# Key and query stores moved to GpSimd's queue, and three loads that are asked for at other places, in a one-core hybrid decoder layer

## The chip, the cores and the metric

One NeuronCore of a Trainium2 chip runs the whole program. The metric is device microseconds of one execution; the kernel was timed in three runs. Five engines work side by side, each through its own list of instructions in order: TensorE (PE; its weight loads are PEld), VectorE (DVE), ScalarE (ACT), GpSimd (POOL) and SyncE (SP), which here only issues transfers. Transfers issued by SP appear in the profile as queue q1 (hardware_dynamic), those issued by GpSimd as queue q0 (software_dynamic).

## The reference

One layer of a decoder with two groups of heads, 1024 tokens behind 16 meta tokens, D_MODEL 1024:

```python
u = rmsnorm(h, attn_norm_w[l])
proj = u @ w_in[l]
gq, gk, gv, gz, gb, ga, fq, fk, fv, ff = jnp.split(proj, IN_SPLITS, axis=-1)
o_gdn = gated_deltanet_group(jnp.concatenate([gq, gk, gv], axis=-1), gz, gb, ga, ...)  # 4 heads, chunked delta rule
o_fox = forgetting_attention_group(fq, fk, fv, ff, fgate_b[l])                         # 8 heads, softmax with forget bias
h = h + jnp.concatenate([o_gdn, o_fox], axis=-1) @ w_out[l]
h = h + swiglu(rmsnorm(h, ffn_norm_w[l]), w_gate[l], w_up[l], w_down[l])
```

and a last rmsnorm. "gdn" below is the delta-rule group, "fox" the attention group.

## The kernel before

Everything is float32 and every matrix product is made of three: each operand is split into a high part (a CAST on ACT, `whi_`, `uh`) and the rest (a subtraction on DVE, `wlo_`, `ul`), by the helper `split`. The stages follow one another on PE; the ones that matter here, with their place in the profiled execution:

- **Value projection** (about 232 to 287 us, tiles `fv`). `fox` goes over two blocks of weights, b = 1 and then 0, and in each over nine token tiles, t = -1 to 7. A tile is 24 matmuls into one of three PSUM banks; ACT and DVE split it into `fvt` (three buffers) and SP stores it to `v_d`. Inside the loop `fox_load` asks for the weights of the next block: it loads two halves (`raw_fv`, then `raw_fk`), and ACT and DVE split them. At the same time DVE inverts 32-row blocks for the delta rule (`invert`, L533 and L535, tile `up`), a long row of small instructions.
- **Key and query projection** (287 to 436 us, tiles `pj_fk` and `pj_fq`). `fox_proj` makes four row blocks m of three pieces each, for keys and then for queries: 24 matmuls, then ACT (L777) and DVE (L778) split the piece into `fhl`, which has two buffers, and L780 stores it to DRAM (`k_d`, `q_d`), whence the attention loads it later. The query pieces are named by their first column, 16, 358 and 700. A piece's ACT instruction waits until the store of the piece two before it has landed, since it writes the same buffer. PE writes the pieces, and after them the `wog` tiles, into three PSUM banks in turn, so that a group of matmuls needs the piece three before it to be split.
- **Delta rule.** In between, `levels` builds the inverses (its loads `ubk` and `na` come from DRAM), and from 349 us on `scan` runs eight chunks: four loads each (`ra`, `rb`, `rc`, `zt`), on PE `p`, `pvn`, `pd`, `po` and `ot`, on DVE `r` (L836) and `s` (L853), on POOL `sg` (L848) and a power for the norm (`os`, L220).
- **Attention** (from 439 us). `att_head` loads a head (`ka`, `qa`, `kk`, `sa`, `avt`, `vm`), PE makes scores (`sc`) in two PSUM banks, DVE (L1030) adds the mask and takes the minimum, ACT exponentiates into `pr` and copies the columns of the meta tokens into `pm` (L1040). As filler between them runs `wout_gdn`: the gdn half of the output projection in tiles `wog`, each with a residual tile `ht` that is loaded from x, added on DVE (L1190) and stored to `h_d`.
- After 666 us come the FFN products, in which PE has no gaps.

PE's order is written by hand through a planner (`PeOrder`, with chains, due times and a filler); the order on the other engines and queues is set when the program is built, by a scheduler that simulates the program and takes `tc.issue_after(x)` as a request that an instruction be placed behind x. A wait at run time comes only from data and from buffers. Each transfer that POOL issues carries one of eight semaphores in turn.

Of the kernel before, what the change touches and what calls it, by code (L numbers as in the profile page):

```python
# [9 lines left out]
F32 = mybir.dt.float32  # L10
# [11 lines left out]
NT = S // P  # L22
# [75 lines left out]
def tile_hymba_layer(ctx, tc, x, meta, attn_norm_w, w_in, conv_w, a_log, dt_bias, gdn_norm_w,  # L98
                     fgate_b, w_out, ffn_norm_w, w_gate, w_up, w_down, final_norm_w, out):
    nc = tc.nc  # L100
    x, out, w_in, conv_w = x[0], out[0], w_in[0], conv_w[0]
# [12 lines left out]
    def ps_mm(name):  # L114
        rot[0] = rot[0] % 3 + 1 if rot[0] else 0
        return ps_v(name) if rot[0] > 1 else bank("mm", 1, name)
# [46 lines left out]
    def split(dst_hi, dst_lo, src, col=None):  # L163
        if col is None:
            cast = nc.scalar.copy(dst_hi, src)  # L165
            low = nc.vector.tensor_sub(dst_lo, src, dst_hi.bitcast(F32))  # L166
        else:
            cast = nc.scalar.activation(dst_hi, src, AF.Copy, scale=col)
            low = nc.vector.scalar_tensor_tensor(dst_lo, src, col, dst_hi.bitcast(F32),
                                                 op0=ALU.mult, op1=ALU.subtract)  # L170
        tail[0] = (cast, low)
        return cast
# [37 lines left out]
    def mm3g(dst, pairs, us):  # L210
        n = len(pairs)
        for i, (lh, ll, rh, rl) in enumerate(pairs):
            for a, b, first, last in ((lh, rh, i == 0, False), (lh, rl, False, False), (ll, rh, False, i == n - 1)):
                nc.tensor.matmul(dst, a, b, start=first, stop=last)  # L214
                od.pe(us)
                yield
# [56 lines left out]
    def tok_cols(t):  # L273
        return (0, NM) if t < 0 else (NM + P * t, P)
# [30 lines left out]
    def gate_out(t, acc, pool, tag, h0):  # L305
        zt = pool.tile([P, 4, 2, DH], F32, tag=tag, name=f"zt{h0}_{t}")
        zt = zt.rearrange("p a b c -> p (a b c)")[:, :256].rearrange("p (h c) -> p h c", h=2)
        nc.scalar.activation(zt, acc[:, :256].rearrange("p (h c) -> p h c", h=2), AF.Silu)
        return nc.sync.dma_start(rec_d[t, :, 7, h0:h0 + 2], zt)
# [291 lines left out]
    def levels(hp):  # L601
        na = lp.tile([P, 2, NT, P], F32, tag="na", bufs=2, name=f"na_{hp}")
        tb = lp.tile([P, 2, NT, 32], F32, tag="tb", bufs=2, name=f"tb_{hp}")
        ubk = lp.tile([P, 2, NT, 32], F32, tag="ubk", bufs=2, name=f"ubk_{hp}")
        with tc.issue_after((last[0] or vst[0]).ins):
            nc.sync.dma_start(ubk, ud_d[hp].rearrange("b j h t k -> (b j) h t k"))
            for i in range(2):
                nc.sync.dma_start(na[:, i], rec_d[:, :, 0, 2 * hp + i].rearrange("t p c -> p t c"))
# [97 lines left out]
    def proj_tmg(acc, t, w, n):  # L706
        col, rows = tok_cols(t)
        yield from mm3g(acc[:rows, :n], [(uh[:, k, col:col + rows], ul[:, k, col:col + rows], w[0][k][:, :n],
                                          w[1][k][:, :n]) for k in range(KT)], n / 2400)

    last, vst = [None], [None]
# [5 lines left out]
    def fox_load():  # L717
        if fox_ws:
            with tc.issue_after(vst[0].ins) if vst[0] and not last[0] else nullcontext():
                fox_w.append(win_block(*fox_ws.pop(0)))  # L720

    t_ld, hds, fixed, fq_m, h_ld = [], {}, [], [0], {}
# [39 lines left out]
    def fox_proj(dst, chunks, off, scale, nm):  # L762
        for b in range(2):
            w = fox_w.pop(0)
            for i in range(2):
                m = 2 * b + i
                for ci, (c0, n) in enumerate(chunks):
                    if (i, ci) == (0, 1):
                        fox_load()
                    acc = ps_mm(f"pj_{nm}{m}_{c0}")  # L770
                    yield from mm3g(acc[:, :n], [(w[0][k][:, P * i:P * i + P], w[1][k][:, P * i:P * i + P],
                                                  uh[:, k, c0:c0 + n], ul[:, k, c0:c0 + n])
                                                 for k in range(KT)], n / 2400)
                    od.on("act", n / 1200)
                    od.on("dve", n / 900)
                    hl = fp.tile([P, 2, 348], F32R, tag="fhl", name=f"fhl_{nm}{m}_{c0}")
                    nc.scalar.activation(hl[:, 0, :n], acc[:, :n], AF.Copy, scale=scale)  # L777
                    nc.vector.scalar_tensor_tensor(hl[:, 1, :n], acc[:, :n], scale, hl[:, 0, :n].bitcast(F32),  # L778
                                                   op0=ALU.mult, op1=ALU.subtract)
                    last[0] = nc.sync.dma_start(dst(m)[:, :, c0 - off:c0 - off + n], hl[:, :, :n].bitcast(F32))  # L780
                    if off:
                        fq_m[0] = m

# [28 lines left out]
    ra_ld = {}  # L812
# [116 lines left out]
    def fox():  # L929
        fox_load()  # L930
        w = fox_w.pop(0)
        for t in range(NT):
            if t == 1:
                fox_load()
            acc = ps_mm(f"z0_{t}")
            yield from proj_tmg(acc, t, w, 256)
            gate_out(t, acc, *((fvp, "fvt") if t < NT - 2 else (fp, "fhl")), 0)
        for b in (1, 0):
            n = 256 + 8 * b
            w = fox_w.pop(0)  # L940
            for t in range(-1, NT):
                if t == 1:
                    fox_load()
                col, rows = tok_cols(t)
                acc = (ps_mm if b or t % 2 else ps_t)(f"fv{b}_{t}")
                yield from proj_tmg(acc, t, w, n)
                vt = fvp.tile([P, 4, 2, DH], F32R, tag="fvt", name=f"fvt{b}_{t}")
                av = acc[:rows, :256].rearrange("p (h d) -> p h d", d=DH)
                split(vt[:rows, :, 0], vt[:rows, :, 1], av)
                src = vt[:rows].rearrange("p h a d -> p h (a d)").bitcast(F32)  # L950
                if t < 0:
                    for j in range(GRP):
                        vst[0] = nc.sync.dma_start(
                            vz_d[4 * b:4 * b + 4, VZ * j:VZ * j + NM * 512].rearrange(
                                "h (r f) -> r h f", f=512)[:, :, 0:P], src)
                else:
                    vst[0] = nc.sync.dma_start(v_d[4 * b:4 * b + 4, col:col + rows].rearrange("h t d -> t h d"), src)
                if b:
                    nc.vector.tensor_copy(fr[:rows, NT if t < 0 else t], acc[:rows, 256:264])
        fvc.close()  # L960
        yield from fox_proj(lambda m: k_d[m], TCH, 0, 1.0, "fk")
        od.add(csum(), od.t + 8.0)
        yield from fox_proj(lambda m: q_d[m].rearrange("a p c -> p a c"), ((NM, 342), (NM + 342, 342), (NM + 684, 340)), NM, -DH ** -0.5, "fq")

    lv_left, outs_left = {0, 1}, set(range(NT))
    for hp in range(2):
        od.add(levels(hp), LV0[hp] - 20.0)
# [179 lines left out]
    h_d = dram.tile([NT, P, D], F32, name="h_d")  # L1147
# [17 lines left out]
    def wout_block(k0, nb, tiles=None, col=None):  # L1165
        ws = ([], [])
        for i in range(2):
            hl = load_w([(wout_w(k0 + 2 * i, nb), 1024)], f"wo{k0}_{nb}{i}", tiles and tiles(i), col)
            for o, t in zip(ws, hl):
                o.extend(t[:, 512 * k:512 * k + 512] for k in range(2))  # L1170
        return ws

    def gdn_pairs(tt, nb):
        a, b, (wh, wl) = og_of("h", tt), og_of("l", tt), wvs[nb]
        return [(a[:, k], b[:, k], wh[k], wl[k]) for k in range(4)]

    def wout_gdn(nb, tt):
        if nb not in wvs:
            parts_n[0] = 2 if nb else 1
            wvs[nb] = wout_block(0, nb, col=gnw)  # L1180
            parts_n[0] = 1
            od.on("act", 2.2)
            od.on("dve", 3.2)
        cols, nbc = slice(P * tt, P * tt + P), slice(512 * nb, 512 * nb + 512)
        ht = wo.tile([P, 512], F32, tag="ht", bufs=5, name=f"ht_{tt}_{nb}")
        with tc.issue_after(ra_ld[NT - 2].ins):
            (nc.gpsimd if len(t_ld) > 1 else nc.sync).dma_start(ht, x[cols, nbc])
        acc = ps_mm(f"wog_{tt}_{nb}")
        yield from mm3g(acc, gdn_pairs(tt, nb), 0.2135)
        V.tensor_add(ht, acc, ht)  # L1190
        nc.gpsimd.dma_start(h_d[tt, :, nbc], ht)
        yield od.on("dve", 0.6)

    tiles = [(nb, tt) for nb in range(2) for tt in range(NT)]
# [96 lines left out]
    with tc.issue_after(ofl[ORDER[1]].ins):  # L1291
        nc.sync.dma_start(nwb2, ffn_norm_w[0].partition_broadcast(P))
    pfp = woc.enter_context(tc.tile_pool(name="pf", bufs=1, side="right", reuse_waits="tile"))
    with tc.issue_after(h_ld[1].ins):
        wfs = [wout_block(4, 0)]
    rot[0] = 1
    for _ in wout_gdn(1, 1):
        pass
# [445 lines left out]
```

## Time and profile before

| | us |
|---|---|
| median of three runs (1304.51 to 1305.75) | 1305.42 |
| the profiled execution | 1304.52 |
| its span | 1302.8 |
| PE busy in the span | 1278.7 |
| DVE / ACT / POOL busy | 837.9 / 547.2 / 352.2 |

Between the span and the time of the profiled execution lie 1.7 us. In a row of the timeline the first number is the start in us, the second the duration, and the bracket at the end tells how long the engine sat idle before the instruction and whose end released it. In a row of the critical chain there is only start, duration and what. "SPq" rows are SP's issues; a row with x4 merges four. The granted clock of PE stands as a share of full speed (PEclk), the DMA share as the mean busy share of the 16 DMA engines.

### The profile page before, as it was taken

To read this page: it belongs to the slowest core of one execution; us is meant where nothing else is said; L and a number is where in the kernel's file an instruction comes from. 1 tells how busy PE (TensorE), PEld (TensorE's weight loads), DVE (VectorE), ACT (ScalarE), POOL (GpSimd) and SP (SyncE) were. 2 spreads that over 40 slices of the span, in tenths; PEclk is the share of its full clock that TensorE was granted. 3 is DMA by queue.
4 is the path that set the end of the run, shared out by engine and by line. 5 is a ranking of instruction groups with operands and counts; after the bars stand their busy time and mean duration, and the time that the engine had idled before them with its cause. 6 is when DMAs were issued, how large, how long until landed. Compare 5 with 4: busy or idle time off the path is not lost.

```text
span 1302.8 us, 19946 instructions
## 1 busy us (share of the span) xinstructions
PE 1278.7 (98%) x7434; PEld 1127.8 (87%) x7434; DVE 837.9 (64%) x1508; ACT 547.2 (42%) x940; POOL 352.2 (27%) x318
## 2 busy tenths in 40 slices
PE   9999999999999799999999999999999999999998
PEld 8999999999999788887778888888888888888887
DVE  6667898573257388886887666556666664365645
ACT  6455444142234377784553333233333343433332
POOL 2012213101222212112504534455334453020401
PEclk9999999999999899999999999999999999999999
DMA  6443624667499867748435644543444467945513
GB/s 230 132 118 110 186 83 106 175 193 221 148 331 258 243 185 190 212 101 258 166 114 161 196 166 157 185 158 134 157 157 162 162 218 264 397 179 193 208 67 129
DMA packets 185808, 234.90 MB, mean 180 GB/s; under 512 B 19160, under 2 KB 137904, under 8 KB 182896
## 3 DMA queue, kind: packets, MB, share of 16 engines
q1 hardware_dynamic: 182576, 224.20, 53.6%
q0 software_dynamic: 3136, 9.44, 2.5%
q8 instruction: 58, 0.95, 0.3%
q14 instruction: 38, 0.31, 0.1%
HBM read 154.68 MB, written 78.92 MB: 179 GB/s over the span
## 4 chain that ended last, share of the span: by engine, by line
PE 89%; DMA 5%; DVE 3%; issue 2%; ACT 1%; SPq 1%; POOL 0%; POOLq 0%; DVEq 0%; ACTq 0%
PE xp L1625 9%; PE yp L1625 7%; PE ua L1450 5%; PE ga L1450 5%; PE gb L1450 5%; PE ud L1450 5%; PE gd L1450 5%; PE ub L1450 5%; PE pj_fk L214 3%; PE pj_fq L214 3%; PE fv L214 2%; PE pt L1071 2%; PE ge L1450 2%; PE ue L1450 2%; PE z L214 2%; PE wog L214 2%
## 5 line engine op out<-in xcount | busy, mean ns | idle before, releaser
L166 DVE TENSOR_TENSOR al_p<-ra_p,ah_p 128x2048 fp32r<-128x2048 f32 (+1 forms) x21 | 46.6, 2221 | 93.8 <-ACT ah_p L165 93.8
L165 ACT CAST ah_p<-ra_p 128x2048 fp32r<-128x2048 f32 (+1 forms) x21 | 37.1, 1766 | 105.9 <-PE xp L1625 48.5
L1625 PE MATMUL xp<-wl_p,ah_p 128*128 128x512 f32 (+1 forms) x176 | 67.3, 382 | 0.0
L1625 PE MATMUL xp<-wh_p,al_p 128*128 128x512 f32 (+1 forms) x176 | 67.3, 382 | 0.0
L1625 PE MATMUL xp<-wh_p,ah_p 128*128 128x512 f32 (+1 forms) x176 | 67.3, 382 | 0.0
L1506 POOL TENSOR_TENSOR gzw<-gzw,uzt 128x512 f32<-128x512 f32 x11 | 18.1, 1650 | 165.2 <-DVE uzt L1495 139.4
L1450 PE MATMUL gb<-uh_p,w_g_p 128*128 128x512 f32 x176 | 57.8, 389 | 0.0
L1450 PE MATMUL gd<-uh_p,w_g_p 128*128 128x512 f32 x176 | 57.8, 389 | 0.0
L1450 PE MATMUL ud<-uh_p,w_u_p 128*128 128x512 f32 x176 | 57.8, 389 | 0.0
L1450 PE MATMUL ub<-uh_p,w_u_p 128*128 128x512 f32 x176 | 57.8, 389 | 0.0
L166 DVE TENSOR_TENSOR w_u_p<-raw_u,w_u_p 128x512 fp32r<-128x512 f32 x42 | 42.9, 1022 | 21.6 <-ACT w_u_p L165 21.5
L1506 POOL TENSOR_TENSOR gxy<-gxy,uxy 128x512 f32<-128x512 f32 x22 | 38.9, 1769 | 65.3 <-DVE uxy L1495 57.5
L165 ACT CAST ph<-pt 128x512 fp32r<-128x512 f32 (+1 forms) x96 | 45.4, 478 | 23.3 <-PE pt L1071 20.7
L166 DVE TENSOR_TENSOR pl<-pt,ph 128x512 fp32r<-128x512 f32 (+1 forms) x96 | 51.9, 552 | 4.5 <-ACT ph L165 4.0
L1035 ACT ACTIVATE pr<-pr,sm 128x144 f32<-128x144 f32 (+3 forms) x64 | 50.7, 793 | 8.1 <-DVE sm L1030 7.7
L1450 PE MATMUL ga<-uh_p,w_g_p 128*128 128x512 f32 x160 | 52.5, 389 | 0.0
L1450 PE MATMUL ua<-uh_p,w_u_p 128*128 128x512 f32 x160 | 52.5, 389 | 0.0
L1625 PE MATMUL yp<-wh_p,ah_p 128*128 128x512 f32 x132 | 51.3, 389 | 0.0
L1625 PE MATMUL yp<-wl_p,ah_p 128*128 128x512 f32 x132 | 51.3, 389 | 0.0
L1625 PE MATMUL yp<-wh_p,al_p 128*128 128x512 f32 x132 | 51.3, 389 | 0.0
L165 ACT CAST w_u_p<-raw_u 128x512 fp32r<-128x512 f32 x42 | 26.1, 620 | 55.4 <-PE gd L1450 33.6
L166 DVE TENSOR_TENSOR wl_p<-rw_p,wh_p 128x2048 fp32r<-128x2048 f32 (+1 forms) x21 | 46.9, 2234 | 3.4 <-ACT wh_p L165 3.4
(649 smaller groups left out, 4235.2 us busy)
## 6 DMA issues: line engine op xcount, KB each, us to landing
ra_p<-ao_p SPq DMA_DIRECT2D x14, 1024.0 KB
raw_g<-in_w_gate_dram SPq DMA_DIRECT2D x22, 512.0 KB
raw_u<-in_w_up_dram SPq DMA_DIRECT2D x22, 512.0 KB
raw_d<-in_w_down_dram SPq DMA_DIRECT2D x22, 512.0 KB
wt_p<-raw_d SPq DMA_DIRECT2D x33, 256.0 KB
rw_p<-wt_p SPq DMA_DIRECT2D x8, 1024.0 KB
rw_p<-in_w_down_dram SPq DMA_DIRECT2D x6, 1024.0 KB
ao_p<-gzw SPq DMA_DIRECT2D x22, 256.0 KB
```

The source lines that it names most:

```text
L165: cast = nc.scalar.copy(dst_hi, src)
L166: low = nc.vector.tensor_sub(dst_lo, src, dst_hi.bitcast(F32))
L214: nc.tensor.matmul(dst, a, b, start=first, stop=last)
L1035: nc.scalar.activation(pr[:, :n], pr[:, :n], AF.Exp, bias=sm[:, np_ - 1:np_], scale=-1.0, accum_out=rsum[:, h, j:j + 1])
L1071: nc.tensor.transpose(pt[:, P * j:P * j + P], pts[j][0][:, j, c0:c0 + P], ident)
L1450: nc.tensor.matmul(dst, a[:, c], b[:, k], start=(first and k == 0 and i == 0), stop=(k == 3 and i == 2), skip_group_check=not first)
L1506: last_mul[0] = G.tensor_tensor(gs[d], gs[d], us[d], op=ALU.mult)
L1625: nc.tensor.matmul(dst[:, n_], a[:, f, c], b[:, f, n_], start=(first and i == 0 and n == 0), stop=(i == NF - 1 and n == 2), skip_group_che ...
```

## The change

- In `fox_proj` the 24 stores of key and query pieces (L780) are issued by GpSimd and no longer by SP.
- In `fox`, in the first value block, the weights of the second are asked for at t = 3 (the fifth tile) and no longer at t = 1.
- In `levels` the three loads are placed behind the last value store that has been written down, no longer behind the last key store.
- In `wout_gdn` the load of a residual tile is placed behind the `h_d` store of the tile two before it. Before, all were placed behind a load of the scan, so that the first five stood together at the start and the others followed as their buffers came free.
- The fox half of the output weights (`wfs`, two loads `raw_wo` of 512 KB) is placed behind the loads of head 2, no longer of head 1.

```diff
--- before.py
+++ after.py
@@ -602,7 +602,7 @@
         na = lp.tile([P, 2, NT, P], F32, tag="na", bufs=2, name=f"na_{hp}")
         tb = lp.tile([P, 2, NT, 32], F32, tag="tb", bufs=2, name=f"tb_{hp}")
         ubk = lp.tile([P, 2, NT, 32], F32, tag="ubk", bufs=2, name=f"ubk_{hp}")
-        with tc.issue_after((last[0] or vst[0]).ins):
+        with tc.issue_after(vst[0].ins):
             nc.sync.dma_start(ubk, ud_d[hp].rearrange("b j h t k -> (b j) h t k"))
             for i in range(2):
                 nc.sync.dma_start(na[:, i], rec_d[:, :, 0, 2 * hp + i].rearrange("t p c -> p t c"))
@@ -777,7 +777,7 @@
                     nc.scalar.activation(hl[:, 0, :n], acc[:, :n], AF.Copy, scale=scale)
                     nc.vector.scalar_tensor_tensor(hl[:, 1, :n], acc[:, :n], scale, hl[:, 0, :n].bitcast(F32),
                                                    op0=ALU.mult, op1=ALU.subtract)
-                    last[0] = nc.sync.dma_start(dst(m)[:, :, c0 - off:c0 - off + n], hl[:, :, :n].bitcast(F32))
+                    last[0] = nc.gpsimd.dma_start(dst(m)[:, :, c0 - off:c0 - off + n], hl[:, :, :n].bitcast(F32))
                     if off:
                         fq_m[0] = m
 
@@ -939,7 +939,7 @@
             n = 256 + 8 * b
             w = fox_w.pop(0)
             for t in range(-1, NT):
-                if t == 1:
+                if t == (3 if b else 1):
                     fox_load()
                 col, rows = tok_cols(t)
                 acc = (ps_mm if b or t % 2 else ps_t)(f"fv{b}_{t}")
@@ -1174,6 +1174,8 @@
         a, b, (wh, wl) = og_of("h", tt), og_of("l", tt), wvs[nb]
         return [(a[:, k], b[:, k], wh[k], wl[k]) for k in range(4)]
 
+    h_st = []
+
     def wout_gdn(nb, tt):
         if nb not in wvs:
             parts_n[0] = 2 if nb else 1
@@ -1183,12 +1185,12 @@
             od.on("dve", 3.2)
         cols, nbc = slice(P * tt, P * tt + P), slice(512 * nb, 512 * nb + 512)
         ht = wo.tile([P, 512], F32, tag="ht", bufs=5, name=f"ht_{tt}_{nb}")
-        with tc.issue_after(ra_ld[NT - 2].ins):
-            (nc.gpsimd if len(t_ld) > 1 else nc.sync).dma_start(ht, x[cols, nbc])
+        with tc.issue_after(h_st[-2].ins) if len(h_st) >= 2 else nullcontext():
+            nc.gpsimd.dma_start(ht, x[cols, nbc])
         acc = ps_mm(f"wog_{tt}_{nb}")
         yield from mm3g(acc, gdn_pairs(tt, nb), 0.2135)
         V.tensor_add(ht, acc, ht)
-        nc.gpsimd.dma_start(h_d[tt, :, nbc], ht)
+        h_st.append(nc.gpsimd.dma_start(h_d[tt, :, nbc], ht))
         yield od.on("dve", 0.6)
 
     tiles = [(nb, tt) for nb in range(2) for tt in range(NT)]
@@ -1291,7 +1293,7 @@
     with tc.issue_after(ofl[ORDER[1]].ins):
         nc.sync.dma_start(nwb2, ffn_norm_w[0].partition_broadcast(P))
     pfp = woc.enter_context(tc.tile_pool(name="pf", bufs=1, side="right", reuse_waits="tile"))
-    with tc.issue_after(h_ld[1].ins):
+    with tc.issue_after(h_ld[2].ins):
         wfs = [wout_block(4, 0)]
     rot[0] = 1
     for _ in wout_gdn(1, 1):
```

No instruction is added or taken away; PE's order is the same row for row. On POOL, between the end of the scan and the start of attention (`ht_0_...` are residual tiles, `q_d<-fhl_fq_16`, `_358` and `_700` the stores of the last five query pieces), it was:

```order
L727 MEMSET ka_4869 6x1040
L728 MEMSET qa_4870 6x1024
L1187 DMA ht_0_5005<-in_x_dram 128x512
L1187 DMA ht_0_5041<-in_x_dram 128x512
L1187 DMA ht_0_5120<-in_x_dram 128x512
L1187 DMA ht_0_5316<-in_x_dram 128x512
L1187 DMA ht_0_5501<-in_x_dram 128x512
L1013 MEMSET zmask 128x1040
L1014 AFFINE_SELECT zmask<-zmask 128x128
L1191 DMA h_d<-ht_0_5005 128x512
```

and is now:

```order
L727 MEMSET ka_4869 6x1040
L728 MEMSET qa_4870 6x1024
L1189 DMA ht_0_5005<-in_x_dram 128x512
L1189 DMA ht_0_5041<-in_x_dram 128x512
L780 DMA q_d<-fhl_fq_358_4826 128x2x342
L780 DMA q_d<-fhl_fq_700_4889 128x2x340
L780 DMA q_d<-fhl_fq_16_4918 128x2x342
L1013 MEMSET zmask 128x1040
L780 DMA q_d<-fhl_fq_358_4947 128x2x342
L1014 AFFINE_SELECT zmask<-zmask 128x128
L780 DMA q_d<-fhl_fq_700_4976 128x2x340
L1193 DMA h_d<-ht_0_5005 128x512
```

Three of the five residual loads have moved behind the `h_d` stores, and five query stores stand where they were and behind the two that stayed.

On DVE at the first chunk of the scan (`r` is its first step on DVE; `fhl_fq` are splits of query pieces), it was:

```order
L778 SCALAR_TENSOR_TENSOR fhl_fk_694_3998<-pj_fk_694_3971,fhl_fk_694_3998 128x346
L778 SCALAR_TENSOR_TENSOR fhl_fq_16_4027<-pj_fq_16_4002,fhl_fq_16_4027 128x342
L778 SCALAR_TENSOR_TENSOR fhl_fq_358_4084<-pj_fq_358_4043,fhl_fq_358_4084 128x342
L836 SCALAR_TENSOR_TENSOR r_4103<-p_0_4098,negegc,ra_4090 128x128 x4
L853 TENSOR_TENSOR s_4158<-pd_4153,sg_4151 128x512
```

and is now:

```order
L778 SCALAR_TENSOR_TENSOR fhl_fk_694_3998<-pj_fk_694_3971,fhl_fk_694_3998 128x346
L778 SCALAR_TENSOR_TENSOR fhl_fq_16_4027<-pj_fq_16_4002,fhl_fq_16_4027 128x342
L836 SCALAR_TENSOR_TENSOR r_4103<-p_0_4098,negegc,ra_4090 128x128 x4
L778 SCALAR_TENSOR_TENSOR fhl_fq_358_4084<-pj_fq_358_4043,fhl_fq_358_4084 128x342
L853 TENSOR_TENSOR s_4158<-pd_4153,sg_4151 128x512
```

The chunk's `r` has moved ahead of the split of the second query piece.

On DVE in the first value block (`wlo_fv` splits the weights of the second, `fvt_2` and `fvt_3` finish its third and fourth full tiles, `up` is the inversion), it was:

```order
L535 TENSOR_REDUCE up_2342<-up_2342 128x8
L166 TENSOR_TENSOR wlo_fv_0_2786<-raw_fv_0_2783,whi_fv_0_2785 128x1024
L533 TENSOR_TENSOR up_2342<-up_2342,ad_2341 128x8x17
L166 TENSOR_TENSOR fvt_2_2850<-fv_2_2825,fvt_2_2850 128x4x64
L959 COPY fr<-fv_2_2825 128x8
L166 TENSOR_TENSOR wlo_fv_1_2792<-raw_fv_1_2789,whi_fv_1_2791 128x1024
L535 TENSOR_REDUCE up_2342<-up_2342 128x8
L166 TENSOR_TENSOR fvt_3_2880<-fv_3_2855,fvt_3_2880 128x4x64
L959 COPY fr<-fv_3_2855 128x8
```

and is now:

```order
L535 TENSOR_REDUCE up_2342<-up_2342 128x8
L533 TENSOR_TENSOR up_2342<-up_2342,ad_2341 128x8x17
L166 TENSOR_TENSOR fvt_2_2838<-fv_2_2813,fvt_2_2838 128x4x64
L959 COPY fr<-fv_2_2813 128x8
L535 TENSOR_REDUCE up_2342<-up_2342 128x8
L533 TENSOR_TENSOR up_2342<-up_2342,ad_2341 128x9x18
L535 TENSOR_REDUCE up_2342<-up_2342 128x9
L533 TENSOR_TENSOR up_2342<-up_2342,ad_2341 128x9x19
L535 TENSOR_REDUCE up_2342<-up_2342 128x9
L533 TENSOR_TENSOR up_2342<-up_2342,ad_2341 128x10x20
L166 TENSOR_TENSOR fvt_3_2880<-fv_3_2855,fvt_3_2880 128x4x64
L959 COPY fr<-fv_3_2855 128x8
```

The tiles' splits no longer stand behind the weights' split: `wlo_fv_0` now comes five rows after the last row shown, just ahead of `fvt_4`.

## The prediction

> **What bounds the kernel now.** I read the page's head, PE's gaps in the timeline, the chain that ended last, and then, around each gap, the rows of the engine named in its bracket. The head:
>
> ```profile
> span 1302.8 us, 19946 instructions
> PE 1278.7 (98%) x7434; PEld 1127.8 (87%) x7434; DVE 837.9 (64%) x1508; ACT 547.2 (42%) x940; POOL 352.2 (27%) x318
> ```
>
> PE is busy in all but 1302.8 − 1278.7 = 24.1 us, and the change leaves its order alone: it can win only PE's gaps and time at a lowered clock. Of the gaps near the changed lines these are the ones that other instructions caused:
>
> ```profile
> 252.15 0.36 PE L214 MATMUL fv<-whi_fv,uh 128*128 128x264 f32 x1 [0.85 <-DVE fr L959]
> 361.66 1.26 PE L841 MATMUL pvn<-r,rb 128*128 128x128 f32 x8 [1.37 <-DVE r L836]
> 446.13 0.80 PE L214 MATMUL wog<-whi_wo,uh_p 128*128 128x512 f32 x1 [6.43 <-DVE fhl_fq L778]
> ```
>
> The last one costs more than its 6.43 us. In the windows (length; busy PE, PEld, DVE, ACT, POOL; PEclk; DMA share; GB/s) the clock drops behind it:
>
> ```profile
> 405.00:410.00 5.00, 5.00 (x41) 5.00 (x40) 4.47 (x12) 2.57 (x4) 1.01 (x1) 1.00 0.66 225
> 424.00:440.00 16.00, 15.70 (x98) 14.96 (x96) 4.54 (x7) 4.07 (x7) 4.74 (x8) 1.00 1.05 249
> 444.00:446.00 2.00, 0.00 (x0) 0.00 (x0) 0.43 (x2) 0.58 (x2) 0.00 (x0) 0.62 1.06 390
> 446.00:448.00 2.00, 1.87 (x5) 1.31 (x6) 1.68 (x7) 1.13 (x4) 0.56 (x1) 0.50 0.96 358
> 450.00:452.00 2.00, 2.00 (x9) 1.83 (x8) 1.01 (x4) 0.74 (x2) 0.55 (x1) 0.68 0.06 21
> ```
>
> A mean of 0.62 over two us puts the fall to 0.50 at 444.5, and 0.68 puts the return at 451.3. PE worked 446.13 to 451.3 at half speed: 5.2/2 = 2.6 us lost. So this place holds 9.0 us. The chain says why:
>
> ```profile
> 435.69 9.31 DMA q_d<-fhl_fq
> 445.08 0.47 ACT fhl_fq L777
> ```
>
> ACT may not rewrite a `fhl` buffer before the query store that reads it has landed; that store took 9.3 us, with the DMA engines at a share above 1.
>
> **The change part by part.** *Value weights at tile five.*
>
> ```profile
> 250.16 1.22 DVE L166 TENSOR_TENSOR wlo_fv<-raw_fv,whi_fv 128x1024 fp32r<-128x1024 f32 x1 [1.69 <-ACT whi_fv L165]
> 250.57 1.05 ACT L165 CAST whi_fv<-raw_fv 128x1024 fp32r<-128x1024 f32 x1 [0.17 <-DMA raw_fv<-in_w_in_dram]
> ...
> 252.15 9.05 PE fv L214 x72
> ```
>
> DVE sat in front of `wlo_fv` until the weights had come, the split of tile 2 stood behind it, and PE found its bank occupied: 0.85 us. Now DVE does that split first. The load comes two tiles later: PE makes three, 72 matmuls, in 9.05, so at most 6.0 us. The second half, which landed at 250.57, then lands by 256.6, its cast (1.05) and subtraction (1.22) end at 258.9, and the next block's weights are needed at 252.15 + 9.05 − 0.85 = 260.35: 1.5 us of slack. Late next could be the split of tile 4, which stands behind the first subtraction and is due about when it ends. I take 0.6 of the 0.85, some of it for that; range −0.5 (such a delay, with the gap gone) to 0.85.
>
> *Stores and the first chunk.*
>
> ```profile
> 351.71 0.55 SPq L780 DMA_DIRECT2D k_d<-fhl_fk  x1
> ...
> 357.52 1.05 PE L832 MATMUL p<-s_m,ra 128*128 128x128 f32 x8
> ...
> 360.12 0.46 ACT L777 ACTIVATE fhl_fq<-pj_fq 128x342 fp32r<-128x342 f32 x1 [3.13 <-DMA k_d<-fhl_fk]
> 360.62 0.52 DVE L778 SCALAR_TENSOR_TENSOR fhl_fq<-pj_fq,fhl_fq 128x342 fp32r<-128x342 f32 x1 [8.30 <-ACT fhl_fq L777]
> ```
>
> A key store took 8.4 us, ACT waited for it, and `r` stood on DVE behind that split, though its input `p` was done by 358.6. Now `r` stands ahead of the split, so the 1.37 us go whatever the store does. Late next: nothing before the bank of the piece three later. I take 1.37; range 0 to 1.37.
>
> *Query stores at the end of the projection.* Before, the stores stood on SP behind head 1's loads:
>
> ```profile
> 411.25 0.33 SPq L823 DMA_DIRECT2D zt<-rec_d  x1
> ...
> 423.10 0.54 SPq L780 DMA_DIRECT2D q_d<-fhl_fq  x1
> ...
> 430.16 5.43 SPq L736 DMA_DIRECT2D vm<-vz_d  x4
> ```
>
> ```profile
> 424.39 2.94 POOL L1187 DMA_DIRECT2D ht<-in_x_dram  x5
> ...
> 429.82 0.46 ACT L777 ACTIVATE fhl_fq<-pj_fq 128x342 fp32r<-128x342 f32 x1 [2.45 <-DMA q_d<-fhl_fq]
> ```
>
> The last two were issued from 435.69 on, after `vm`. Now all follow their splits on POOL, but the first, that of `fhl_fq_358` of the third row block, stands behind two memsets and two `ht` loads and is issued near 425.7 instead of 423.10. How fast does q0 carry it? Its rows there, and those of the `h_d` stores as a contrast (landing times for the group above them; the two rows between are of 424 to 440):
>
> ```profile
> L1187 POOL DMA_DIRECT2D ht<-in_x_dram x5: 546/546/770, 424.4 to 426.8; - x5
> DMA to landing us min/median/max: 6.3/9.4/12.9
> q1 hardware_dynamic: 1828, 2.67, 69.6%
> q0 software_dynamic: 400, 1.31, 35.4%
> L1191 POOL DMA_DIRECT2D h_d<-ht x10: 553/564/592, 447.0 to 593.4; - x10
> DMA to landing us min/median/max: 2.3/4.4/7.9
> ```
>
> The five landed from 424.4 + 6.3 = 430.7 to 426.8 + 12.9 = 439.7: one per 2.25 us, for 256 KB each. A query piece (342 KB) then takes 3.0 us in that queue; the bounds are 2.3 (the quickest `h_d`, 256 KB) and 7.9 (the slowest). I take 3.0, as the loads are the nearest in place and share. Behind two loads (second landing 433.0) the stores land at 436.0, 439.0 and 442.0. The first frees ACT's `fhl` 16 at 436.0 (429.82 before): PE's first `wog` is reached at 436.3 and waits until 437.0, 0.7 us new. The second frees 358, split at 440.0, just before PE reaches the second `wog`. The third frees 700, split at 443.05, and on DVE stand behind it the `ht` add and the first mask:
>
> ```profile
> 446.00 0.68 DVE L1190 TENSOR_TENSOR ht<-wog,ht 128x512 f32<-128x512 f32 x1
> 446.59 0.29 DVE L1030 CUSTOM_DVE_ANT_0 pr<-sc,zmask 128x144 f32<-128x144 f32 x1
> 447.15 0.54 PE L1025 MATMUL sc<-ka,qa 70*128 70x400 f32 x1
> ```
>
> Add until 443.75, mask until 444.05, and the scores of 400 columns that PE began at 447.15 begin there: gain 3.1. With an interval of d it is 433.0 + 3d + 2.05, so the range is −11.6 (d of 7.9) to 6.0, where PE itself is the limit. These times are on the clock of before; the pile-up as a whole starts with head 0's loads, which SP issues behind `zt` at 411.25 once the scan frees its buffer, and at 405 to 410 the DMA share is only 0.66. So it moves forward with the scan, and the 2.0 of the two terms above are kept.
>
> *The clock.* PE's idle stretch shrinks to about 3.3 us. The 1.37 us at 361 left it at 1.00 (the window of 350 to 415, below), and the fall came 444.5 − 439.7 = 4.8 us after the last matmul:
>
> ```profile
> 439.41 0.29 PE L1026 MATMUL sc<-kk,sa 128*128 128x272 f32 x1
> ```
>
> Between the two nothing shows: I take half of 2.6, 1.3, range 0 to 2.6. [...]
>
> *A new wait in attention.* ACT's `pm` copy now waits for the two last query stores on their POOL semaphores, the later of them on its way at that time. It ran at
>
> ```profile
> 453.80 0.23 ACT L1040 COPY pm<-pr 128x64 f32<-128x64 f32 x1
> ```
>
> and the last store, split at 443.05, issued at 443.6, lands by 448.0 like the median `h_d` or 451.5 like the slowest; with PE 4.4 us ahead the copy wants to run at 449.4. I take −0.4, near the median; range −2.1 to 0.
>
> *At nothing.* POOL's issues:
>
> ```profile
> 290.00:350.00 60.00, 60.00 (x700) 56.90 (x699) 22.17 (x38) 18.50 (x33) 9.21 (x10) 1.00 0.52 164
> 350.00:415.00 65.00, 63.63 (x500) 62.15 (x499) 39.26 (x121) 23.09 (x40) 14.58 (x15) 1.00 0.90 304
> ```
>
> 24 issues at an `h_d`'s 0.56 are 13.5 us beside POOL's 9.2 and 14.6; without that cover each could hold a scan power up by 0.56, 6.7 us over the twelve query stores. SP loses as many issues. The loads of `levels` come earlier, under a PE that is busy 60.00 of 60 at a DMA share of 0.52. The later `ht` loads are issued two `h_d` stores ahead, and those ten are spread over 146 us, about 16 apart, so a landing of 12.9 fits; were they 10 apart on PE's path, DVE's add would wait the rest. The fox weights, 1 MB:
>
> ```profile
> 440.05 2.63 SPq L182 DMA_DIRECT2D raw_wo<-in_w_out_dram  x2
> ...
> 469.40 1.96 SPq L736 DMA_DIRECT2D vm<-vz_d  x2
> ...
> 521.74 1.05 ACT L165 CAST whi_wo<-raw_wo 128x1024 fp32r<-128x1024 f32 x1 [0.67 <-PE wog L214]
> ```
>
> leave the crowded stretch; issued behind head 2's last load (`vm`, until 471.4), they have 50 us until they are cast.
>
> Sum: 0.6 + 1.37 + 3.1 + 1.3 − 0.4 = 6.0. The profiled execution took 1304.52, so 1298.5; it lies 0.9 below the median of the runs, 1305.42, and I forecast a median of 1299.0 (rounded down from 1299.4, as the `ht` and `raw_wo` bytes leave the stretch).
>
> **The rivals.**
>
> *The whole gap goes.* If q0 is served beside q1 and not after its own loads, each store lands 4.4 us after its issue, as the median `h_d`. Then no store is late, the 400 columns begin as PE reaches them, near 441.2, gain 6.0, the clock stays (2.6), and with 2.0 and −0.4 it is 10.2: 1304.5 − 10.2 + 0.9 = 1295.2. For it: three `ht` loads (768 KB) and 1 MB of weights leave the stretch. Against: 1.05 of share from 424 to 440. Chance 0.25.
>
> *Nothing at the gap.* Bytes set the landing, not the queue: the two queues have 69.6% and 35.4%, more than all engines together, and the last piece lands at 445 by whichever. Left are 0 to 2.2 us of the first two terms, less the new wait: 1303.2 to 1305.4, middle 1304.3. [...] Chance 0.20.
>
> *Slower: the stores follow one another on q0 slowly.* At 7.9 us each behind the loads they land at 440.9, 448.8 and 456.7, and the 400 columns begin at 433.0 + 23.7 + 2.05 = 458.75, 11.6 later; less the other terms' 1.6 (the clock falls as before) it is 10.0: 1315.4. It decides from d = (447.15 + 1.6 − 435.05)/3 = 4.6 us, and the kernel is measurably slower, by 2.6, from 5.4 on. For it: a query store reads 256 rows where a load has 128. Against: the loads' 2.25. Chance 0.10.
>
> The forecast itself: 0.45, own range 1296.5 to 1302.
>
> **How the numbers follow.** About 0.2% (2.6 us) is what a measurement can tell from no change: faster is below 1302.8, slower above 1308. Forecast and full recovery are faster, 0.70; "nothing" is the same, 0.20; slower 0.10. The range goes from 1294.0, below the full recovery's 1295.2 by the 0.85 and the 0 at the ends of two terms, to 1304.5, the middle of "nothing"; outside lie the slower case and half of that one's chance.
>
> **What would show it.** Value loop: no gap at 252, `wlo_fv` behind `fvt_3`. Scan: `pvn` at once after `p`, `r` ahead of the split. End of the projection: the rows of L777 on ACT with their releasers, the landing time of POOL's `q_d` from 424 on, and PE's idle before the second `wog` and the 400 columns, with PEclk from 440 to 452 at 1.00 or 0.50. I'm wrong if the landings there are 5 us apart or more, if POOL's powers in the scan show idle ends behind L780, or if `pm` waits for `q_d`.

## The result, and the profile after

The changed kernel takes 1297.51 us, the median of four runs (1296.40 to 1298.46), beside 1304.97 for the kernel before in the same comparison: ratio 0.9947, 95% interval 0.9935 to 0.9959, so about 6.9 us (5.3 to 8.5) faster. The forecast was 1299.0 with a range of 1294.0 to 1304.5. Timed once more with the last experiments it gave 1297.52. The profiled execution took 1297.96, against 1304.52 before: 6.56 less. The page's head:

```profile
span 1296.2 us, 19960 instructions
PE 1276.9 (99%) x7434; PEld 1125.5 (87%) x7434; DVE 840.6 (65%) x1508; ACT 546.6 (42%) x940; POOL 367.2 (28%) x342
```

PE's idle time fell from 24.1 to 19.3 us, and its busy time by 1.8 us with the same matmuls. PE's rows in the timeline that answer to those before, and the 400 columns:

```profile
241.96 0.36 PE L214 MATMUL fv<-whi_fv,uh 128*128 128x264 f32 x1 [0.45 <-DVE up L535]
...
436.97 0.50 PE L214 MATMUL wog<-whi_wo,uh_p 128*128 128x512 f32 x1 [3.00 <-DVE fhl_fq L778]
...
442.59 0.45 PE L1025 MATMUL sc<-ka,qa 70*128 70x400 f32 x1
```

The gaps at 252 and 361 are gone, and of the 6.43 us 3.00 are left, now before the first `wog` tile and no longer before the second. The windows (columns as before) show the clock behind it:

```profile
436.00:438.00 2.00, 1.03 (x4) 0.88 (x5) 1.50 (x3) 2.00 (x5) 0.67 (x1) 0.97 0.77 173
438.00:440.00 2.00, 2.00 (x6) 1.52 (x5) 2.00 (x4) 1.16 (x2) 1.73 (x3) 0.50 0.58 218
440.00:442.00 2.00, 2.00 (x9) 1.67 (x9) 1.12 (x3) 0.45 (x1) 0.50 (x3) 0.67 0.46 175
```

One minus PEclk, times length, times two gives 2 × 2 × (0.03 + 0.50 + 0.33) = 3.4 us at half clock, 1.7 us lost, against 6.8 us before, of which 2.6 were lost with PE at work. The profile of before has one more stretch of 3.4 us at half clock, at 11 us, which the changed one lacks. It is part of the 1.8 us of busy time but not of the gain: by 18 us PE is only 0.2 us ahead. The ledger of the two profiles:

| | before | after | won |
|---|---|---|---|
| first `wog` reached by PE | 436.30 | 433.97 | 2.3 |
| PE's wait at the two `wog` tiles | 6.43 | 3.00 | 3.4 |
| lost at half clock | 2.6 | 1.7 | 0.9 |
| span | 1302.8 | 1296.2 | 6.6 |

GpSimd's timeline at the end of the projection, and then the chain:

```profile
424.24 1.16 POOL L1189 DMA_DIRECT2D ht<-in_x_dram  x2 [2.38 <-issue]
425.47 1.45 POOL L780 DMA_DIRECT2D q_d<-fhl_fq  x2
```

```profile
425.47 10.34 DMA q_d<-fhl_fq
...
435.91 0.47 ACT fhl_fq L777
```

The groups of the stores by their line, first with the landing times of all 24, then those of the last five:

```profile
L780 POOL DMA_DIRECT2D k_d<-fhl_fk x12: 666/687/877, 295.4 to 349.4; - x12
L780 POOL DMA_DIRECT2D q_d<-fhl_fq x12: 719/746/791, 351.6 to 441.9; - x12
DMA to landing us min/median/max: 2.8/4.4/10.3
```

```profile
DMA to landing us min/median/max: 3.0/3.3/10.3
```

Two stores have to be kept apart here. Before, PE's long wait hung on the store of piece 700 of the third row block, which was split by 427.4 and issued at 435.69. That store is now issued at 426.19, 9.5 us earlier, and takes no less time: 9.99 us, not 9.31. The store that PE waits for now is the one ahead of it, of piece 358: on SP it was issued at 423.10 and had landed by 429.8; on GpSimd it stands behind two memsets and two loads, is issued at 425.47 and lands at 435.81.

### The profile page after: what moved, and what is told of

It is laid out like the page before. It is cut to its first block, busy times and chain, and to the rows that moved or that the text cites. A ratio compares the mean times of both kernels' runs of the same rounds, so it can differ in the third digit from the quotient of the medians.

```text
span 1296.2 us, 19960 instructions
## 1 busy us (share of the span) xinstructions
PE 1276.9 (99%) x7434; PEld 1125.5 (87%) x7434; DVE 840.6 (65%) x1508; ACT 546.6 (42%) x940; POOL 367.2 (28%) x342
## 4 chain that ended last, share of the span: by engine, by line
PE 90%; DMA 4%; DVE 2%; issue 2%; POOL 1%; SPq 1%; ACT 1%; POOLq 0%; DVEq 0%; ACTq 0%
PE xp L1627 9%; PE yp L1627 7%; PE ua L1452 5%; PE ga L1452 5%; PE gb L1452 5%; PE ud L1452 5%; PE gd L1452 5%; PE ub L1452 5%; PE pj_fk L214 4%; PE fv L214 3%; PE pt L1071 2%; PE ue L1452 2%; PE ge L1452 2%; PE wog L214 2%; PE z L214 2%
```

## The experiments

Ratios are to the kernel before, run in the same group; an interval of 0.0025 is about 3.2 us wide. Three groups of four were timed: e1 to e4, e5 to e8, e9 to e12. "Queue theory" holds that a query store is late by what stands ahead of it on its own queue; "byte theory", that the traffic of all queues on the shared DMA engines sets it.

### The value weights alone (e1)

```diff
-                if t == 1:
+                if t == (3 if b else 1):
                     fox_load()
```

> The kernel before with one part of the change alone: the value weights asked for at tile five. Theory (the win passes on): the 0.85 us gap at 252 goes, PE reaches the first wog tile about 1.0 us earlier, and the pile-up of transfers moves with it, so the time falls by 0.6 to 1.0 us, ratio 0.9993. Rival (swallowed): the query store lands when it did, PE's wait before the second wog grows from 6.43 to about 7.4 us and the time stays, ratio 1.000.

1303.31 us, ratio 0.9998 (0.9989 to 1.0007). PE and SP in its timeline:

```profile
445.01 0.80 PE L214 MATMUL wog<-whi_wo,uh_p 128*128 128x512 f32 x1 [6.88 <-DVE fhl_fq L778]
...
435.98 2.08 SPq L780 DMA_DIRECT2D q_d<-fhl_fq  x2
```

The gap at 252 goes and PE reaches the first `wog` 1.6 us sooner (434.73), but SP issues the awaited stores at 435.98, where it did before (435.69), and the wait grows by 0.45. So the 0.6 are not a sum that stands by itself: with the stores on SP part of it runs into the wait, and the time can't tell the rest from nothing.

### Stores back on SP (e2), and stores on GpSimd alone (e3)

e2 is the changed kernel, e3 the kernel before, each with this line exchanged:

```diff
-                    last[0] = nc.gpsimd.dma_start(dst(m)[...], hl[...])
+                    last[0] = nc.sync.dma_start(dst(m)[...], hl[...])
```

(in e3 the other way).

> The changed kernel with the 24 key and query stores issued by SP again, all other parts kept. Queue theory (a query store is late by what stands in front of it on its queue): the last stores stand behind head 1's avt and vm again and r stands behind the split of the second query piece, so of the change only the value weights' 1 us and some relief by 0.75 MB fewer residual loads is left: a wait of 4.5 to 6.5 us before the second wog, the clock at 0.50 behind it, 1301 to 1304 us. Byte theory (the residual loads that left the crowded stretch made the gain, whichever queue): the wait stays near 3.0 us and the time is within 1.5 us of the changed kernel's 1297.5.

> The kernel before with the 24 stores issued by GpSimd and nothing else changed: the query stores of the end now stand behind five residual loads instead of two. Queue theory: the 1.37 us at the scan's first chunk go, but the 0.75 MB more in front of the first store cost it about 5 us at the 0.13 MB per us that GpSimd's queue carried from 428 to 436 in the changed kernel; it lands near 441, PE waits about 7 us before the first wog, and the time is 1303 to 1306, no gain. Rival (the store's own queue is all that matters): the first store lands near 436 as in the changed kernel, 1299 to 1300 us.

e2: 1302.72 us, 0.9992 (0.9983 to 1.0001). e3: 1301.64 us, 0.9981 (0.9972 to 0.9989). PE's gaps in the timeline of e2, and its chain:

```profile
441.41 0.79 PE L214 MATMUL wog<-whi_wo,uh_p 128*128 128x512 f32 x1 [3.47 <-DVE fhl_fq L778]
...
444.16 0.70 PE L1025 MATMUL sc<-ka,qa 70*128 70x400 f32 x1 [1.53 <-DVE sm L1030]
```

```profile
424.55 8.75 DMA sa<-q_d
433.37 6.90 DMA q_d<-fhl_fq
```

Without the stores' move nearly all of the gain is gone, though 0.75 MB of residual loads are still out of the stretch: the byte theory's 1297.5 is excluded. The store whose piece was split at 427 is issued at 433.37, behind a load that SP waited for. For e3, its gap and GpSimd's issues in the timeline:

```profile
440.06 0.79 PE L214 MATMUL wog<-whi_wo,uh_p 128*128 128x512 f32 x1 [5.25 <-DVE fhl_fq L778]
...
425.17 2.76 POOL L1187 DMA_DIRECT2D ht<-in_x_dram  x5 [2.48 <-issue]
427.92 0.75 POOL L780 DMA_DIRECT2D q_d<-fhl_fq  x1
```

e3 came out between the two expectations: the 1.37 us at the scan's first chunk are gone, and the store behind five loads landed near 438.9, 11.0 us after its issue. The stores' move alone is worth 2.5 us (1.4 to 3.7), all the rest without it 1.0 (−0.1 to 2.2), both together 6.9: neither half carries the gain by itself.

### Five residual loads first (e5), and the weights early (e8)

Both are the changed kernel with one part undone.

```diff
e5
-        with tc.issue_after(h_st[-2].ins) if len(h_st) >= 2 else nullcontext():
-            nc.gpsimd.dma_start(ht, x[cols, nbc])
+        with tc.issue_after(ra_ld[NT - 2].ins):
+            (nc.gpsimd if len(t_ld) > 1 else nc.sync).dma_start(ht, x[cols, nbc])
e8
-    with tc.issue_after(h_ld[2].ins):
+    with tc.issue_after(h_ld[1].ins):
```

> The changed kernel with the residual loads placed as before, so that five of them stand on GpSimd in front of the query stores. Queue theory: as with the stores alone moved, the first store is issued near 427.5 and lands near 438.5, PE waits 4.5 to 5.5 us before the first wog instead of 3.0 and the clock is low for two stretches of 3.4 us instead of one: 1300 to 1302 us. Rival (what stands in front on GpSimd's queue is nothing beside the traffic of SP's): 1297 to 1298, as the changed kernel.

> The changed kernel with the fox output weights (1 MB) behind head 1's loads again, as before. If moving them was worth nothing: 1297 to 1298, the stores landing as in the changed kernel. Rival (their bytes slow the third store and the loads of the crowded stretch): the third query store, issued at 437, lands 2 us later or more, a wait before the 400 columns, 1299 to 1301 us.

e5: 1299.02 us, 0.9961 (0.9948 to 0.9973). e8: 1297.32 us, 0.9950 (0.9938 to 0.9963), no different from the changed kernel. e5's gap in PE's timeline, and its chain:

```profile
438.02 0.58 PE L214 MATMUL wog<-whi_wo,uh_p 128*128 128x512 f32 x1 [4.20 <-DVE fhl_fq L778]
```

```profile
426.48 10.39 DMA q_d<-fhl_fq
```

With three more loads ahead the store is issued 1.0 us later and lands 1.1 later (436.9, not 435.8): it takes 10.39 us behind five loads and 10.34 behind two. So the 0.75 MB ahead cost this store only the time to issue them. (The second store lost more: it was issued at 433.62, not 426.19, 0.33 us after the second load had landed, and so it was in e3, at 434.89. The profile names no releaser that explains it, and PE did not wait for it.) That contradicts the queue theory, by which they should have cost some 5 us. The loads' place is worth 1.2 us in the gap; in the time it is 1.8 us against the changed kernel's 0.9947, with some 2.3 of uncertainty from the two intervals, no more than a hint. The weights' place is worth nothing that shows in the time, though e8's profile has a wait of 1.91 us before the 400 columns, as the rival had it, beside 2.32 before the first `wog`.

### Where the two residual loads stand (e4, e6)

```diff
e4: behind the two query stores on GpSimd (q_st lists the stores)
-        with tc.issue_after(h_st[-2].ins) if len(h_st) >= 2 else nullcontext():
+        with tc.issue_after(h_st[-2].ins if len(h_st) >= 2 else q_st[-4].ins):
e6: on SP, behind head 1's loads
+        with tc.issue_after(h_st[-2].ins if len(h_st) >= 2 else ra_ld[NT - 1].ins):
+            (nc.gpsimd if len(h_st) >= 2 else nc.sync).dma_start(ht, x[cols, nbc])
```

> The changed kernel with the first two residual loads placed on GpSimd behind the two query stores that they stand in front of. Queue theory: those 0.5 MB cost the first store about 4 us; without them it lands near 431.5 instead of 435.8, the wait of 3.0 us before the first wog goes and the clock stays at 1.00: a gain of up to 3.0 + 1.7 = 4.7 us over the changed kernel, 1292.8 to 1294.5. Byte theory (the loads of heads 0 and 1 on SP's queue starve GpSimd's whatever its order): the first store lands at 434.5 or later and the time is 1296 to 1298.

> The changed kernel with the first two residual loads issued by SP behind head 1's loads, so that GpSimd's queue holds only stores. Queue theory: the third store, which landed 7.8 us after its issue behind those two loads when they stood in the middle, lands within 5 to 6 us, PE finds no wait at either wog and none before the 400 columns, the clock stays at 1.00: 1291 to 1293 us. Rival: the engines are full, so the loads' bytes delay the stores from SP's queue just as well, or the loads themselves land late and DVE's add waits for them: 1294 to 1297 us.

e4: 1295.32 us, 0.9935 (0.9922 to 0.9947). e6: 1297.17 us, 0.9942 (0.9930 to 0.9954). Of e4 the timeline (PE's gap and ACT's split) and the chain, then of e6 PE's gap in the timeline and the chain:

```profile
439.07 0.45 PE L1026 MATMUL sc<-ka,qa 70*128 70x400 f32 x1 [1.96 <-DVE sm L1031]
...
427.85 0.46 ACT L777 ACTIVATE fhl_fq<-pj_fq 128x342 fp32r<-128x342 f32 x1 [4.04 <-DMA q_d<-fhl_fq]
```

```profile
429.25 7.84 DMA q_d<-fhl_fq
```

```profile
440.23 0.70 PE L1025 MATMUL sc<-ka,qa 70*128 70x400 f32 x1 [2.74 <-DVE sm L1030]
```

```profile
429.96 8.29 DMA q_d<-fhl_fq
```

In both the first store goes at 421.3 to 421.6, lands in 6.5 to 6.8 us, and the wait before the first `wog` is gone. The second store, issued at 424.3 and 424.8 with no load ahead on its queue, takes 6.9 and 7.2 us, where it took 9.99 behind two loads in the changed kernel. So two loads ahead go with some 3 us, near the 4 of the queue theory; but the store also goes 1.4 to 1.9 us earlier here, and what that is worth is not separated. Then the third store becomes the late one, 7.8 us with two loads ahead of it on its queue and 8.3 us with none. For this one the queue's own content doesn't set the landing, and the expected full recovery (1291 to 1294.5) failed on it.

### Head 1's loads out of the way (e9)

```diff
-        nc.sync.dma_start(vt.bitcast(F32), v_d[h, NM:T].rearrange("(t p) d -> p t d", p=P))
+        if h == 1:
+            vm_load(0)
+            h1.append(lambda: (...))    # avt_1 in two halves and vm_1, by nc.gpsimd
...
+        with tc.issue_after(last[0].ins):    # behind the last query store
+            h1.pop()()
```

> The changed kernel with two of head 1's loads, avt (512 KB) and its vm (256 KB), taken off SP and placed on GpSimd behind the last query store, where they have some 20 us until head 1 needs them. Byte theory (what SP's queue carries beside them sets how long a store takes): with 0.75 MB less at some 250 KB per us the first store, issued near 425, lands about 3 us sooner than 435.8, PE's wait before the first wog falls from 3.0 to under 1 us and the clock stays at 1.00: 1293 to 1295 us. Rival (a store issued there takes 10 us whatever else is moved): it lands at 435 or later, 1296.5 to 1298 us.

1296.13 us, 0.9937 (0.9924 to 0.9949). PE's gaps in the timeline, the chain, and a window:

```profile
435.12 0.50 PE L214 MATMUL wog<-whi_wo,uh_p 128*128 128x512 f32 x1 [1.64 <-DVE fhl_fq L784]
...
440.30 0.45 PE L1033 MATMUL sc<-ka,qa 70*128 70x400 f32 x1 [1.20 <-DVE sm L1038]
```

```profile
425.05 8.90 DMA q_d<-fhl_fq
```

```profile
434.00:436.00 2.00, 0.89 (x4) 0.75 (x5) 0.87 (x2) 1.30 (x3) 0.53 (x1) 1.00 0.01 5
```

The store lands after 8.90 us instead of 10.34, and the engines are empty as soon as it has landed. So the traffic of SP's queue is part of what holds the store, in the direction of the byte theory, at half of its 3 us; the clock stayed at 1.00 up to 1291 us. The time lies between the two expectations, 1.4 us below the changed kernel's of the same group, which is within the noise.

### A third buffer (e7, e10, e12)

```diff
-                    hl = fp.tile([P, 2, 348], F32R, tag="fhl", name=f"fhl_{nm}{m}_{c0}")
+                    hn[0] += 1
+                    hl = (fp3[0] if hn[0] % 3 == 0 else fp).tile([P, 2, 348], F32R, tag="fhl", ...)
...
-        oc = cp.tile([P, GH, P], F32, tag="oc", bufs=2, name=f"oc_{t}")
+        oc = cp.tile([P, GH, P], F32, tag="oc", bufs=1, name=f"oc_{t}")
```

`fp3` is one more buffer of the same size. e7 is the changed kernel with it, e10 the kernel before with it, and e12 is e7 with e4's place of the loads.

> The changed kernel with three buffers for the split pieces instead of two (and one instead of two for the scan's copy of its output, to make room), so that ACT waits for the store three pieces back. If the landing of the stores is all that is left at the end of the projection, the 3.0 us and the low clock go: a gain of 4 to 5 us, 1292.5 to 1293.5 us. Rival: the next wait stands right behind it, the residual loads for DVE's add or the loads of head 0, or the scan's single buffer costs it back: 1295 to 1298 us.

> The kernel before with the third buffer alone (and the scan's single output buffer that makes room for it); the stores stay on SP behind head 1's loads and five residual loads stand at the start. If the wait for the landing of the stores is what the end of the projection cost, not where the stores are issued, the 6.43 us and the 2.6 us at half clock go here too, and perhaps the 1.37 us at the scan's first chunk: 1294 to 1296.5 us, ratio 0.992 to 0.994. Rival: the transfers behind that wait (residual tiles, head 0's loads) are late as well, and a wait of 3 us or more appears at DVE's first add: 1299 to 1302 us.

> The changed kernel with both the third buffer and the two residual loads placed behind the query stores. If the third buffer already took all of the wait, the place of the loads is worth nothing any more: 1293 to 1294.5 us, as with the buffer alone. Rival: the earlier stores free the attention's copy (pm, which waited 0.57 us for a query store with the buffer alone) and later stages too: 1291.5 to 1292.5 us.

e7: 1293.61 us, 0.9922 (0.9909 to 0.9936). e10: 1303.51 us, 0.9993 (0.9984 to 1.0002). e12: 1293.30 us, 0.9913 (0.9899 to 0.9926). ACT and PE in e7's timeline, then PE's gap in e10's and its chain:

```profile
427.05 0.46 ACT L780 ACTIVATE fhl_fq<-pj_fq 128x342 fp32r<-128x342 f32 x1 [3.17 <-PE pj_fq L214]
...
438.25 0.45 PE L1029 MATMUL sc<-ka,qa 70*128 70x400 f32 x1
```

```profile
445.83 0.70 PE L1029 MATMUL sc<-ka,qa 70*128 70x400 f32 x1 [7.72 <-DVE sm L1034]
```

```profile
434.40 9.45 DMA q_d<-fhl_fq
```

In e7 ACT waits for PE and no longer for a store, PE runs through, and the time is 3.3 us below the changed kernel's by the ratios (0.9922 beside 0.9947), a little less than the 4 to 5 that were expected. e10 is the clear miss of this study: with the stores on SP the buffer alone wins nothing. The second of the late stores, whose piece was split by 424, is issued at 434.40 behind head 1's loads, lands at 443.9, and the wait only moves to the 400 columns, 7.72 us. Of the kernels run here only those with both, prompt issue and a third buffer, have no wait left: the changed kernel's issue alone leaves 3 us, the buffer alone 7.7. e12 is the fastest kernel run here, but not clear of e7. It shows the loads' place once more: its store of piece 700, issued at 424.03 ahead of the two loads, takes 5.41 us, e7's, issued at 425.62 behind them, 9.32.

### The changed kernel again (e11)

> The changed kernel once more, unaltered, timed beside the other runs of this group: 1296.5 to 1298.5 us. Its wait at the end of the projection should again stand before the first wog, near 3 us, with one or two stretches of 3.4 us at half clock; how much those differ from the first profile tells how much of a difference between two kernels is the phase of the clock's stretches.

1297.52 us, 0.9945 (0.9932 to 0.9957), with waits

```profile
436.53 0.50 PE L214 MATMUL wog<-whi_wo,uh_p 128*128 128x512 f32 x1 [2.54 <-DVE fhl_fq L778]
...
442.28 0.45 PE L1025 MATMUL sc<-ka,qa 70*128 70x400 f32 x1 [0.18 <-DVE sm L1030]
```

and one stretch of 3.4 us at half clock. Waits of two executions of one kernel differ here by a few tenths of a us (3.00 beside 2.54 and 0.18).

## Why the prediction was right, point by point

**The whole.** 6.0 us were forecast, 6.56 measured between the profiles. The bytes that left the stretch don't carry it (e2), nor does the stores' move alone (e3: 2.5 us); the sum needs both. The rivals "the whole gap goes" and "nothing at the gap" are both excluded by the 3.00 us that stayed of 6.43, and the slower one by the sign. (The upper end of the range, 1304.5, is called the middle of "nothing", whose sum gave 1304.3; nothing hangs on it.)

**Value weights, 0.6.** The gap of 0.85 went, and PE starts the key projection 1.34 us sooner (285.07, not 286.41), of which another 0.15 is a shorter gap at 242. But e1 shows that this passes on only where the late stores move with PE. The prediction kept it because the pile-up starts behind the scan; for SP's stores that was wrong (435.98 in e1, 435.69 before), for GpSimd's it held: e5, which has over e3 the value weights' place and those of the loads of `levels` and of the fox weights, reaches the first `wog` 1.0 us sooner (433.82, not 434.81), issues the store 1.4 us sooner (426.48, not 427.92) and waits 1.05 us less.

**First chunk, 1.37.** Right, and by the reason given. DVE after:

```profile
357.58 1.13 DVE L836 SCALAR_TENSOR_TENSOR r<-p,negegc,ra 128x128 f32<-128x128 f32 x4 [6.36 <-DMA zt<-rec_d]
358.62 0.51 DVE L778 SCALAR_TENSOR_TENSOR fhl_fq<-pj_fq,fhl_fq 128x342 fp32r<-128x342 f32 x1
```

PE is busy 15.00 of 15 us from 350 to 365, where it was 13.63. Of these 2.7 us in all, 2.3 reached the first `wog`. Most of what is missing went at the second chunk's `ot`, whose input `on` DVE makes in four instructions. First before, then after:

```profile
380.95 1.94 DVE L878 SCALAR_TENSOR_TENSOR on<-oc,os,zt 128x128 f32<-128x128 f32 x4
```

```profile
377.92 0.79 POOL L780 DMA_DIRECT2D q_d<-fhl_fq  x1 [1.08 <-DVE os L875]
...
378.10 2.37 DVE L878 SCALAR_TENSOR_TENSOR on<-oc,os,zt 128x128 f32<-128x128 f32 x4
...
378.73 1.05 POOL L848 TENSOR_TENSOR sg<-s,egl 128x512 f32<-128x512 f32 x1
```

The second of the four ends some 0.15 us after GpSimd's `sg` in both profiles, and a store's issue now stands ahead of `sg`. PE's lead falls there from 2.86 to 2.48 us. The row is 2.37 us in all ten profiles with the stores on GpSimd and 1.94 in the four with them on SP, so the stores cause it; how is not shown.

**The query stores, 3.1.** Near in size (the wait fell by 3.43), wrong in its working, so that the size is partly luck. The step that failed is the queue's rate: stores 3.0 us apart behind the loads, the first at 436.0, the third deciding. Measured, the first landed at 435.81 and the second 0.4 us later (10.34 and 9.99 us after issue), the third 3.0 us after its own issue at 437.33. So the wait stood at the first `wog`, 3.00 where 0.7 was forecast, and none was left before the 400 columns, where 3.3 were. That the 436.0 was met is luck: with the 2.0 us that the stretch was to move forward it meant 434 here, and the store landed 1.8 us after that, issued behind a hold of 2.38 us ahead of the first load, which the profile gives to no releaser. A fixed time per transfer in the queue is not what the runs show: e5's store takes 10.39 us behind five loads, e6's third 8.3 behind none, while the second store gains some 3 to 4 us where the two loads don't stand ahead of it (e4, e6, e12). What holds the store from 424 to 436 is in part SP's traffic, as the two queues in the changed kernel suggest, first from 424 to 428, then from 428 to 432:

```profile
q1 hardware_dynamic: 214, 0.68, 73.3%
q0 software_dynamic: 42, 0.16, 23.8%
```

```profile
q0 software_dynamic: 155, 0.51, 50.4%
q1 hardware_dynamic: 201, 0.48, 48.5%
```

How the engines share themselves between two queues stays open; e9 explains 1.4 of the 10.3 us.

The move saved no transfer time (for the store of piece 700 9.31 us before, 9.99 after), only the time until it was issued, which was 9.5 us for this store.

**The clock, 1.3.** 0.9 measured. The half of 2.6 was a guess between two cases, and the case was a loss of one stretch instead of two (3.42 us at half clock, not 6.82).

**The copy `pm`, −0.4.** It ran without a wait in the changed profile, and waited 0.66 us for a query store in e11; PE shows no gap for it in either. The prediction has this wait both as a term and as a sign of being wrong; as a sign it came, in e11, without a cost that shows.

**At nothing.** GpSimd's stores took 0.69 and 0.75 us each, not 0.56, some 17 us in all. No gap of PE follows one, but the cover did not hold throughout: the 0.4 us at `ot`, above, is what the term put at nothing cost. The weights' place is worth nothing that can be measured (e8: 0.9950 beside 0.9947). The `levels` loads were not tried alone.

## What to carry to other kernels

When an engine waits for a store to land, look first at when the store was issued against when its data was ready: the 8 us that a store stood behind loads on one issuing engine (split by 427.4, issued at 435.69) don't show in the transfer's own row. Moving the issue can make another store late: here the one ahead of it (landed by 429.8 before, at 435.81 after). Then ask whether a buffer would take the wait away, and try both together, since either alone can leave the wait standing one piece earlier or later (3.00 us in the changed kernel, 7.72 in e10 with the buffer alone, none in e7 with both). A gain ahead of a wait that ends on a transfer counts only if that transfer moves with it (in e1 it was issued at 435.98, not 435.69, and the ratio stayed at 0.9998).

## What the runs showed of the hardware that was not expected

The time at half clock in the crowded stretch came to 3.40 to 3.42 us, or to two or three times that, in every profile that has any. By the same sum over windows as above, beside PE's waits there:

| kernel | waits, us | at half clock, us |
|---|---|---|
| before | 6.43 | 6.82 |
| changed, twice | 3.00; 2.54 and 0.18 | 3.42; 3.42 |
| e1 | 6.88 | 6.82 |
| e2 | 3.47 and 1.53 | 10.22 |
| e3 | 5.25 | 6.82 |
| e4 | 1.96 | 3.42 |
| e5 | 4.20 | 3.42 |
| e6 | 2.74 | 6.82 |
| e8 | 2.32 and 1.91 | 3.40 |
| e9 | 1.64 and 1.20 | 0 |
| e10 | 7.72 | 10.24 |
| e7, e12 | none | 0 |

The prediction had a wait of 3.3 us between 1.37 us, which left the clock at 1.00, and 4.8 us, after which it fell to 0.50. In these runs the length of a wait doesn't tell by itself whether the clock falls. It fell behind 1.91 us before the 400 columns in e8 and behind 1.96 us in e4, while it stayed at 1.00 behind e8's 2.32 us before the first `wog` and behind e9's 1.64 and 1.20 us. Nor does it tell for how long: 2.74 us in e6 went with 6.82 us at half clock, 3.00 us in the changed kernel and 4.20 in e5 with 3.42.

What a stretch cost here went with how much PE worked in it: e1's 6.82 us cost 1.6 us of work, the same length before 2.6. In e2 one more stretch, 3.42 us, came at 354 to 358 with no wait of PE ahead of it, right behind the small matmuls for the meta tokens. So a wait of PE is not all that goes ahead of such a stretch; what else sets it is not shown.
